# Second MLP of a hybrid decoder layer: the down projection as seven products of block sums for each 512 inner rows

## Chip, cores, metric

One core of a Trainium2 chip. The metric is the device time of one execution in microseconds, from the first to the last instruction and a little around it. Lower is better.

## Reference

One layer of a decoder, for a prompt of 2048 tokens and 32 sample tokens: an input projection with dilated attention and a state-space scan, an output projection, a cross-attention, an MLP and a final norm. What the change touches is the MLP alone:

```python
x = x + jnp.square(jax.nn.relu(rmsnorm(x, g_mlp) @ w_up)) @ w_down   # w_up 1024 x 4096, w_down 4096 x 1024
y = rmsnorm(x, g_final)
```

All data are float32. Every matmul operand is split into a high part and a low remainder, and a product is made of three matmuls: high x high, low x high, high x low.

## The kernel before

After attention and the scan, `Trunk.run` handles the tokens in two groups, one after the other: 1024 tokens (g = 0), then 1056 (g = 1, with the sample tokens). Data lie transposed: 128 features on the partitions, tokens along the free dimension. The second group's tokens are cut into three tiles of 352 (`cs`).

The MLP runs over f = 0 to 15, 256 inner rows each, and j = 0, 1. `up(f, j)` makes 128 inner rows: for each token tile 24 matmuls (`gemm`: 8 blocks of the feature dimension, three each) into a PSUM bank of the tag "g" (four banks), then `act`: DVE scales and clips (L2022), ACT squares (L2023, the high part `us[f, j, 0]`), POOL squares again (L2024) and DVE subtracts (L2025, the low part `us[f, j, 1]`), three tiles later by `line.later(3, ...)`. Then, one f behind, the half j of `down(f - 1)`: for each of four blocks m of 128 output features and each of three token tiles six matmuls (L2034 to L2036) into one of four PSUM banks (three of the tag "a", one "s", in turn), and DVE adds the bank to the running sum `xs[m]` in SBUF (L2044; L2041 and L2042 for f = 0).

`Stream` (`W`) brings the weights: `blocks()` lists them in the order of their use, 128 x 1024 values each. `load` starts the DMA from SP into one of two buffers `w_raw`; `scale` multiplies the up blocks by the norm's gain on POOL (L1335); `split` makes the parts in two halves of 512, high on ACT (`w_hi`, L1291), low on DVE (`w_lo`, L1292), into one of two buffers each. `W.next(wait)` hands out a block, starts the load of the block after the next, and through `line.later` puts the two halves of the next block's split after the tiles number `wait` and `wait + 1` of the work that begins (`line.tick()` counts tiles). `up` uses `wait` 1, `down` uses 4. Within an engine the order of the instructions is the order in which this code issues them; across engines only data and free buffers make one wait.

In the first group the attention over the sample tokens' cache (`samples`, with products on POOL in L2247 and sums on DVE in L2234) runs beside the MLP, in steps between tiles, and the down banks are three.

Of the kernel before, what the change touches and what calls it, by code (L numbers as in the profile page):

```python
# [18 lines left out]
P = 128  # L19
# [1296 lines left out]
class Stream:  # L1316


    def __init__(self, E, pool, line, blocks):
        self.E, self.pool, self.line, self.blocks = E, pool, line, list(blocks)  # L1320
        self.raw, self.parts, self.i = {}, {}, 0
        self.load(0)
        self.load(1)

    def load(self, i):
        if i < len(self.blocks):
            src, gain = self.blocks[i]
            k = src.shape[1]
            t = self.raw[i] = self.pool.tile([P, k, 1024 // k], F32, name="w_raw", tag="w_raw", bufs=2)
            self.E.nc.sync.dma_start(t, src)  # L1330

    def scale(self, i):
        if i < len(self.blocks) and self.blocks[i][1] is not None:
            t = self.raw[i]
            self.E.nc.gpsimd.tensor_tensor(t, t, self.blocks[i][1][:, :, None].to_broadcast([P, 8, P]), op=ALU.mult)  # L1335

    def split(self, i, half=None):

# [81 lines left out]
class Trunk:  # L1420
# [25 lines left out]
    def blocks(self):  # L1446
        E = self.E

        def cut(w, c, gain):
            return w.rearrange("(k p) f -> p k f", p=P)[:, :, c:c + P], gain  # L1450

        for g in range(2):
            for m in range(4):
                yield cut(E.w_in[0], 1536 + m * P, self.gm)
            for w in (E.w_mk, E.w_mv) if g == 0 else ():
                for m in range(8):
                    yield cut(w[0], m * P, None)
# [6 lines left out]
            for f in range(17):
                for j in range(2):
                    if f < 16:
                        yield cut(E.w_up[0], 256 * f + P * j, self.gu)
                    if f:
                        yield (E.w_down[0][256 * (f - 1):256 * f, 512 * j:512 * j + 512]
                               .rearrange("(k p) f -> p k f", p=P), None)  # L1470
# [36 lines left out]
    def run(self):  # L1507
# [46 lines left out]
        def group(g, tail):  # L1554
# [460 lines left out]
                    while rb2 is not None and pss:  # L2015
                        act(f, j, *pss.pop(0))

            def act(f, j, s, ps):
                k = s.stop - s.start
                t1 = small()  # L2020
# [6 lines left out]
            def down(f, m, s, w):  # L2027
# [22 lines left out]
            for f in range(16):  # L2050
                for j in range(2):
                    up(f, j)
                    if g == 0 and f == 15 and j:
# [393 lines left out]
```

## Time and profile before

| | |
|---|---|
| median of 3 runs | 3468.25 us (3466.62 to 3468.25) |
| the profiled execution | 3462.61 us, span 3460.8 us |
| PE (TensorE matmul) busy | 3297.6 us, 95% of the span |
| DVE, ACT, POOL busy | 56%, 34%, 37% |
| the second group's MLP | about 2690 to 3416 us of the span |

The trace shows for each instruction when it began and how long it took, on which engine and from which line; PEld is the weight load before a matmul. A matmul's shown duration overlaps with the next one's, so what a matmul costs is read from the distance between the starts of neighbours. "Idle before" names what ended an engine's wait. The granted clock is the share of TensorE's full clock that it was given.

### The profile page before, as it was taken

To read this page: it belongs to the slowest core of one execution; us is meant where nothing else is said; L and a number is where in the kernel's file an instruction comes from. 1 tells how busy PE (TensorE), PEld (TensorE's weight loads), DVE (VectorE), ACT (ScalarE), POOL (GpSimd) and SP (SyncE) were. 2 spreads that over 40 slices of the span, in tenths; PEclk is the share of its full clock that TensorE was granted. 3 is DMA by queue.
4 is the path that set the end of the run, shared out by engine and by line. 5 is a ranking of instruction groups with operands and counts; after the bars stand their busy time and mean duration, and the time that the engine had idled before them with its cause. 6 is when DMAs were issued, how large, how long until landed. Compare 5 with 4: busy or idle time off the path is not lost. (4 is left out here: it accounts for less than half of the span.)

```text
span 3460.8 us, 52997 instructions
## 1 busy us (share of the span) xinstructions
PE 3297.6 (95%) x20631; PEld 2926.6 (85%) x20631; DVE 1949.4 (56%) x3946; ACT 1186.5 (34%) x2764; POOL 1271.4 (37%) x1025
## 2 busy tenths in 40 slices
PE   9999998999789999899999999989999999999998
PEld 7999997777577887677776777889889999999998
DVE  5334887777664334577754455563334455555555
ACT  5443555778353333211111111344433311111113
POOL 1114555478423334766411122543324522112213
PEclk9999999999899999999999999999999999999999
DMA  7669454456772211455335423712431222222222
GB/s 205 208 192 253 102 129 142 135 142 162 222 202 71 61 49 57 166 191 198 131 127 180 158 83 111 263 40 86 128 110 37 92 98 92 96 81 98 92 96 83
DMA packets 406429, 447.25 MB, mean 129 GB/s; under 512 B 39932, under 2 KB 338607, under 8 KB 402594
## 3 DMA queue, kind: packets, MB, share of 16 engines
q1 hardware_dynamic: 375986, 384.08, 35.8%
q0 software_dynamic: 27744, 44.57, 4.8%
q10 hardware_dynamic: 2448, 15.21, 1.3%
q8 instruction: 163, 2.67, 0.3%
q14 instruction: 88, 0.72, 0.1%
HBM read 368.33 MB, written 142.44 MB: 148 GB/s over the span
## 5 line engine op out<-in xcount | busy, mean ns | idle before, releaser
L1502 PE MATMUL g_g<-g_b,w_hi 128*128 128x352 f32 (+1 forms) x1760 | 629.3, 359 | 14.8 <-ACT w_hi L1291 14.8
L1503 PE MATMUL g_g<-g_b,w_lo 128*128 128x352 f32 (+1 forms) x1760 | 621.5, 355 | 9.7 <-DVE w_lo L1292 9.7
L2024 POOL TENSOR_TENSOR g_small<-g_small 128x352 f32<-128x352 f32 (+1 forms) x160 | 143.6, 898 | 960.0 <-ACT g_a L2023 955.1
L1292 DVE TENSOR_TENSOR w_lo<-w_raw,w_hi 128x512 fp32r<-128x512 f32 x400 | 350.3, 881 | 193.2 <-ACT w_hi L1291 192.5
L1291 ACT ACTIVATE w_hi<-w_raw 128x512 fp32r<-128x512 f32 x400 | 241.1, 622 | 611.3 <-issue 354.3
L2034 PE MATMUL g_a<-g_a,w_hi 128*128 128x352 f32 (+3 forms) x1076 | 391.2, 364 | 21.7 <-DVE g_a L2044 17.8
L1502 PEld LDWEIGHTS g_g<-g_b,w_hi 128*128 128x128 f32 x1760 | 335.3, 191 | 61.4 <-ACT w_hi L1291 20.4
L2035 PE MATMUL g_a<-g_a,w_lo 128*128 128x352 f32 (+3 forms) x1076 | 385.1, 358 | 2.0 <-DVE w_lo L1292 2.0
L2036 PE MATMUL g_a<-g_a,w_hi 128*128 128x352 f32 (+3 forms) x1076 | 383.8, 357 | 0.9 <-DVE g_a L2025 0.9
L1503 PEld LDWEIGHTS g_g<-g_b,w_lo 128*128 128x128 f32 x1760 | 335.1, 190 | 41.9 <-DVE w_lo L1292 12.1
L1505 PE MATMUL g_g<-g_b,w_hi 128*128 128x352 f32 (+1 forms) x1760 | 366.7, 350 | 0.5 <-DMA g_b<-s_xl 0.5
L2044 DVE TENSOR_TENSOR g_a<-g_a,g_a 128x512 f32<-128x512 f32 (+2 forms) x504 | 292.5, 591 | 107.6 <-PE g_a L2036 106.4
L1505 PEld LDWEIGHTS g_g<-g_b,w_hi 128*128 128x128 f32 x1760 | 304.8, 188 | 31.1 <-DMA g_b<-s_xl 1.0
L2023 ACT ACTIVATE g_a<-g_small 128x352 fp32r<-128x352 f32 (+1 forms) x160 | 87.9, 551 | 635.4 <-DVE g_small L2022 635.4
L2022 DVE SCALAR_TENSOR_TENSOR g_small<-g_g,g_rb 128x352 f32<-128x352 f32 (+1 forms) x160 | 94.2, 589 | 317.0 <-PE g_g L1505 285.9
L2034 PEld LDWEIGHTS g_a<-g_a,w_hi 128*128 128x128 f32 x1076 | 202.8, 188 | 68.7 <-DVE g_a L2044 30.0
L1502 PE MATMUL g_g<-g_a,w_hi 128*128 128x352 f32 (+1 forms) x632 | 226.6, 359 | 6.5 <-ACT g_a L1571 4.6
L1503 PE MATMUL g_g<-g_a,w_lo 128*128 128x352 f32 (+1 forms) x632 | 224.4, 356 | 3.3 <-DVE w_lo L1292 3.3
L2036 PEld LDWEIGHTS g_a<-g_a,w_hi 128*128 128x128 f32 x1076 | 203.2, 189 | 23.7 <-DVE g_a L2025 1.4
L2035 PEld LDWEIGHTS g_a<-g_a,w_lo 128*128 128x128 f32 x1076 | 202.9, 189 | 22.7 <-DVE w_lo L1292 2.9
L1039 ACT ACTIVATE w_spare<-w_spare,t_stats 128x256 f32<-128x256 f32 (+1 forms) x376 | 168.7, 450 | 65.6 <-DVE t_stats L1037 65.3
L2025 DVE TENSOR_TENSOR g_a<-g_small,g_a 128x352 fp32r<-128x352 f32 (+1 forms) x160 | 186.8, 1169 | 2.6 <-POOL g_small L2024 2.4
(470 smaller groups left out, 6878.6 us busy)
## 6 DMA issues: line engine op xcount, KB each, us to landing
w_raw<-in_w_up_dram SPq DMA_DIRECT2D x64, 512.0 KB
w_raw<-in_w_down_dram SPq DMA_DIRECT2D x64, 512.0 KB
out_dram<-in_cache_win_k_dram SPq DMA_DIRECT2D x32, 1022.0 KB
out_dram<-in_cache_win_v_dram SPq DMA_DIRECT2D x32, 1022.0 KB
g_wide<-in_cache_win_k_dram SPq DMA_DIRECT2D x32, 512.0 KB
t_cf<-s_coef SPq DMA_DIRECT2D x32, 384.0 KB
g_spare<-in_cache_win_v_dram SPq DMA_DIRECT2D x48, 256.0 KB
a_xn<-in_x_prompt_dram SPq DMA_DIRECT2D x16, 512.0 KB
```

The lines of the kernel that those rows point to most:

```text
L1039: nc.scalar.activation(pr[:, u, :w], pr[:, u, :w], AF.Exp, bias=nm, scale=-1.0, accum_out=stats[:, 1, u, col:col + 1])
L1291: nc.scalar.activation(hi, src, AF.Copy)
L1292: nc.vector.tensor_tensor(lo, src, hi.bitcast(F32), op=ALU.subtract)
L1502: mm(ps[:, :n], hi[:, k], rhs[0][k][:, s], start=first and k == ks[0], stop=False)
L1503: mm(ps[:, :n], lo[:, k], rhs[0][k][:, s], start=False, stop=False)
L1505: mm(ps[:, :n], hi[:, k], rhs[1][k][:, s], start=False, stop=last and k == ks[-1])
L2024: nc.gpsimd.tensor_tensor(t1[:, :k], t1[:, :k], t1[:, :k], op=ALU.mult)
L2025: line.later(3, lambda: nc.vector.tensor_tensor(ul[:, s], t1[:, :k], uh[:, s].bitcast(F32), op=ALU.subtract))
L2034: mm(ps[:, :k], hi[:, j, c], us[f, j, 0][:, s], start=(j == 0), stop=False)
L2035: mm(ps[:, :k], lo[:, j, c], us[f, j, 0][:, s], start=False, stop=False)
L2036: mm(ps[:, :k], hi[:, j, c], us[f, j, 1][:, s], start=False, stop=(j == 1))
L2044: nc.vector.tensor_tensor(xs[m][:, s], xs[m][:, s], ps[:, :k], op=ALU.add)
```

## The change

Only the second group's MLP changes, and there f = 0 to 13. Two f are taken together as 512 inner rows. With the inner rows in two halves, the output features in two halves (512 each) and the tokens in two halves (528 each), the product is one of 2 x 2 by 2 x 2 blocks, which takes seven block products and a number of block sums instead of eight products. f = 14 and 15 stay as they were.

- `blocks()` yields, for each round of 512 inner rows, four up blocks and seven down blocks, in the order up, 1, 2, up, 5, 6, 3, up, 7, up, 4. Blocks 5, 6, 3 and 7 are sums or differences of quarters of the weights: `sums` makes them on POOL, two operations of 512 columns each, in place in `w_raw`, from the block before (`last`) or from two more halves that `load` brings into `extra`.
- `W.next` makes the sum of the next block before the load that would overwrite its source.
- `squares(p, j)` takes the place of `up`: the same matmuls, the same scaling on DVE and the square on ACT, but for p < 7 the square is kept whole, and POOL's square and DVE's subtraction fall away.
- `begin` and `rest_of` make the differences of token halves and inner halves on POOL (`combine`, 528 columns an operation); `prepare` splits an operand into its parts, high on ACT, low on POOL.
- `product(ends, shared)` is one of the seven: 4 blocks of 128 output features x 2 tiles of 264 tokens, six matmuls each, into the same four banks; DVE adds the bank to each of the running sums named in `ends`, and for blocks 1 and 6 to a sum `common`, which three quarters of the output get at the end. Blocks 1, 5 and 7 so have two targets for each bank.
- `whole` puts the residual into `xs` on POOL during the first round, where f = 0 did it with its first addition.
- The split of a next block's halves stands after the first and the second tile in `product` (`wait` 1).

The running sums and prepared operands lie in tiles that the MLP of the second group did not use. The number of matmuls goes from 14 x 144 = 2016 of 352 columns to 7 x 7 x 48 = 2352 of 264 columns.

```diff
+                else:
+                    for f in range(8):
+                        for j, then in enumerate(("12", "563", "7", "4")):
+                            yield cut(E.w_up[0], 512 * f + P * j, self.gu)
...
+    def sums(self, i, kind):
+        t = self.raw[i]
+        for k in range(2):
+            d = t[:, k]
+            o = self.last[:, k] if kind in "63" else self.extra[k]
+            a, b = (o, d) if kind == "6" else (d, o)
+            op = ALU.add if kind == "5" else ALU.subtract
+            self.E.nc.gpsimd.tensor_tensor(d, a, b, op=op)
+        self.last = t
...
         self.split(i)
+        if wait is not None:
+            self.scale(i + 1)
         self.load(i + 2)
...
+                def prepare(src):
+                    hi, lo = sets[ready[0] % 2]
+                    ready[0] += 1
+                    for k in range(2):
+                        nc.scalar.activation(hi[:, k].bitcast(F32R), src[k], AF.Copy)
+                        nc.gpsimd.tensor_tensor(lo[:, k].bitcast(F32R), src[k], hi[:, k], op=sub)
...
+                def product(ends, shared=None, hooks={}):
+                    hi, lo = W.next()
+                    bh, bl = (t.bitcast(F32R) for t in sets[turn[0] % 2])
...
+                    for i in range(8):
+                        m, c = divmod(i, 2)
+                        f, t = slice(P * m, P * m + P), slice(264 * c, 264 * c + 264)
+                        ps = psum("aaas"[i % 4])[:, :264]
+                        for k in range(2):
+                            mm(ps, hi[:, k, f], bh[:, k, t], start=k == 0, stop=False)
+                            mm(ps, lo[:, k, f], bh[:, k, t], start=False, stop=False)
+                            mm(ps, hi[:, k, f], bl[:, k, t], start=False, stop=k == 1)
+                        line.tick()
+                        for mh, th in ends:
+                            o = 528 * th + 264 * c
+                            add_to(xs[4 * mh + m][:, o:o + 264], ps)
...
+                    squares(p, 0, {0: [lambda: prepare(part(old, 1, 0))]})
+                    product([(0, 0)], "first" if p == 1 else "more")
+                    product([(0, 0)], None, {1: [lambda: prepare(both(ta))]})
+                    squares(p, 1, {0: [lambda: prepare(both(tb))], 1: [lambda: W.scale(W.i + 1)],
+                                   2: [lambda: rest_of(old)]})
+                    product([(0, 1), (1, 1)], None, {6: [lambda: W.scale(W.i + 1)]})
+                    product([], "more", {1: [lambda: prepare(part(old, 1, 1))]})
+                    product([(0, 1)], None, {1: [lambda: prepare(both(tb))]})
+                    squares(p, 2, {0: []})
+                    product([(1, 0), (1, 1)], None, {1: []})
+                    squares(p, 3, {0: [lambda: prepare(both(ta))]})
+                    product([(1, 0)], None, {1: [lambda: begin(new)] if p < 7 else [],
+                                             4: [lambda: prepare(part(new, 0, 0))] if p < 7 else []})
```

On DVE, before: the end of an up and the begin of a down half. L2022 is the scaling of a tile, L2025 the low part of the squares, L2044 the addition of a bank (g_a_..., g_s_...) to a running sum (g_a04 is `xs[4]`), L1292 half of a w_lo.

```order
L2022 SCALAR_TENSOR_TENSOR g_small_25799<-g_g_25772,g_rb2_24954 128x352
L2022 SCALAR_TENSOR_TENSOR g_small_25828<-g_g_25803,g_rb2_24954 128x352
L2025 TENSOR_TENSOR g_a13_25738<-g_small_25768,g_a12_25737 128x352
L2044 TENSOR_TENSOR g_a04_25415<-g_a04_25415,g_s_25835 128x352
L2025 TENSOR_TENSOR g_a13_25738<-g_small_25799,g_a12_25737 128x352
L2044 TENSOR_TENSOR g_a04_25415<-g_a04_25415,g_a_25844 128x352
L2025 TENSOR_TENSOR g_a13_25738<-g_small_25828,g_a12_25737 128x352
L2044 TENSOR_TENSOR g_a04_25415<-g_a04_25415,g_a_25853 128x352
L1292 TENSOR_TENSOR w_lo_25870<-w_raw_25735,w_hi_25869 128x512
L2044 TENSOR_TENSOR g_a05_25449<-g_a05_25449,g_a_25862 128x352
```

The same place on DVE now: the end of a `squares` (L2178 is its scaling) and the begin of product 1. L2123 is the addition; g_sum is `common`.

```order
L2178 SCALAR_TENSOR_TENSOR g_small_24867<-g_g_27213,g_rb2_24977 128x352
L2178 SCALAR_TENSOR_TENSOR g_small_24868<-g_g_27242,g_rb2_24977 128x352
L1292 TENSOR_TENSOR w_lo_27280<-w_raw_27175,w_hi_27279 128x512
L2123 TENSOR_TENSOR g_a00_24872<-g_a00_24872,g_a_27272 128x264
L2123 TENSOR_TENSOR g_sum_24886<-g_sum_24886,g_a_27272 128x264
L1292 TENSOR_TENSOR w_lo_27280<-w_raw_27175,w_hi_27279 128x512
L2123 TENSOR_TENSOR g_a00_24872<-g_a00_24872,g_a_27285 128x264
L2123 TENSOR_TENSOR g_sum_24886<-g_sum_24886,g_a_27285 128x264
L2123 TENSOR_TENSOR g_a01_24873<-g_a01_24873,g_a_27296 128x264
L2123 TENSOR_TENSOR g_sum_24886<-g_sum_24886,g_a_27296 128x264
```

The w_lo halves have moved from behind the third addition of a half to ahead of the first two tiles' additions, and each bank is now read twice.

On POOL, before: one f and a half of the second group. L2024 is the square of a tile, L1335 the scaling of an up block.

```order
L2024 TENSOR_TENSOR g_small_27828<-g_small_27828 128x352
L2024 TENSOR_TENSOR g_small_27859<-g_small_27859 128x352
L2024 TENSOR_TENSOR g_small_27888<-g_small_27888 128x352
L1335 TENSOR_TENSOR w_raw_27795<-w_raw_27795,g_gu_7428 128x1024
L2024 TENSOR_TENSOR g_small_28034<-g_small_28034 128x352
L2024 TENSOR_TENSOR g_small_28065<-g_small_28065 128x352
L2024 TENSOR_TENSOR g_small_28094<-g_small_28094 128x352
L1335 TENSOR_TENSOR w_raw_28001<-w_raw_28001,g_gu_7428 128x1024
```

On POOL now, from product 2 to product 6 of one round: L2120 is the low part of a prepared operand (g_wide is a prepared set or `ta`, g_sum is `tb`), L1346 a block sum, L2113 a difference (`rest_of`), L1358 the scaling.

```order
L1358 TENSOR_TENSOR w_raw_25382<-w_raw_25382,g_gu_7428 128x1024
L2120 TENSOR_TENSOR g_wide_24881<-g_wide_24884,g_wide_24880 128x528 x2
L1346 TENSOR_TENSOR w_raw_25465<-w_raw_25465,g_small_24870 128x512
L1346 TENSOR_TENSOR w_raw_25465<-w_raw_25465,g_small_24871 128x512
L2120 TENSOR_TENSOR g_wide_24883<-g_sum_24885,g_wide_24882 128x528 x2
L1346 TENSOR_TENSOR w_raw_25543<-w_raw_25465,w_raw_25543 128x512 x2
L2113 TENSOR_TENSOR g_wide_24884<-g_a12_25094,g_sum_24885 128x528
L2113 TENSOR_TENSOR g_wide_24884<-g_a13_25188,g_sum_24885 128x528
L2113 TENSOR_TENSOR g_sum_24885<-g_a12_25094,g_a10_24891 128x528
L2113 TENSOR_TENSOR g_sum_24885<-g_a13_25188,g_a11_25000 128x528
L1346 TENSOR_TENSOR w_raw_25644<-w_raw_25644,w_raw_25543 128x512 x2
L2120 TENSOR_TENSOR g_wide_24881<-g_a12_25094,g_wide_24880 128x528
```

POOL's three squares for each up are gone, and a row of operations on two SBUF tiles has taken their place.

## Rows read from the trace of the kernel before

**Rows 1.** The page's first part: busy time of each engine, share of the span, instructions.

```profile
PE 3297.6 (95%) x20631; PEld 2926.6 (85%) x20631; DVE 1949.4 (56%) x3946; ACT 1186.5 (34%) x2764; POOL 1271.4 (37%) x1025
```

**Rows 2.** Busy time by stretch: the begin of the second group's MLP, and its steady part.

```profile
core 0: us, PE busy (x) PEld busy (x) DVE busy (x) ACT busy (x) POOL busy (x), PEclk, DMA share, GB/s
...
2690.00:2744.00 54.00, 49.94 (x293) 47.80 (x292) 22.84 (x38) 17.89 (x28) 22.47 (x22) 0.97 0.24 79
2744.00:3395.00 651.00, 650.99 (x4056) 650.69 (x4055) 364.32 (x618) 107.47 (x198) 139.24 (x127) 1.00 0.27 91
```

**Rows 3.** Groups of instructions by line in 2744 to 3395: line, engine, operation, out<-in, form, count | busy us, mean ns | idle before, what ended it.

```profile
L2044 DVE TENSOR_TENSOR g_a<-g_a,g_a 128x352 f32<-128x352 f32 x243 | 121.9, 514 | 36.0 <-PE g_a L2036 35.8
...
L2025 DVE TENSOR_TENSOR g_a<-g_small,g_a 128x352 fp32r<-128x352 f32 x84 | 89.3, 1063 | 0.0
L1292 DVE TENSOR_TENSOR w_lo<-w_raw,w_hi 128x512 fp32r<-128x512 f32 x113 | 83.3, 737 | 36.8 <-ACT w_hi L1291 36.8
L1291 ACT ACTIVATE w_hi<-w_raw 128x512 fp32r<-128x512 f32 x113 | 67.9, 624 | 263.9 <-issue 179.2 <-POOL w_raw L1335 84.7
L2024 POOL TENSOR_TENSOR g_small<-g_small 128x352 f32<-128x352 f32 x85 | 65.9, 775 | 510.2 <-ACT g_a L2023 510.2
L1335 POOL TENSOR_TENSOR w_raw<-w_raw,g_gu 128x1024 f32<-128x1024 f32 x28 | 61.0, 2180 | 0.0
```

**Rows 4.** The first group's MLP, timeline (start us, duration us, engine, line): a w_lo beside a POOL product, the addition behind it, and PE.

```profile
1504.24 2.84 POOL L2247 TENSOR_TENSOR g_spare<-g_wide,g_spare 128x1024 f32<-128x1024 f32 x1
...
1505.35 2.28 DVE L1292 TENSOR_TENSOR w_lo<-w_raw,w_hi 128x512 fp32r<-128x512 f32 x1
...
1507.56 0.67 DVE L2044 TENSOR_TENSOR g_a<-g_a,g_a 128x512 f32<-128x512 f32 x1
...
1508.28 0.50 PE L2034 MATMUL g_a<-g_a,w_hi 128*128 128x512 f32 x1 [0.58 <-DVE g_a L2044]
1508.62 0.39 PE L2035 MATMUL g_a<-g_a,w_lo 128*128 128x512 f32 x1
```

**Rows 5.** The first group's MLP in three views: busy time of 1470 to 1710 (columns as in rows 2); PE's waits there (us in total, times, longest); DVE's groups by line in 1440 to 1700.

```profile
1470.00:1710.00 240.00, 225.17 (x950) 176.23 (x949) 180.25 (x199) 35.71 (x60) 152.36 (x70) 1.00 0.53 178
...
PEld g_a L2034 <- DVE g_a L2044: 22.9, 21, 1.6
...
L1292 DVE TENSOR_TENSOR w_lo<-w_raw,w_hi 128x512 fp32r<-128x512 f32 x43 | 52.8, 1229 | 13.4 <-ACT w_hi L1291 13.4
...
L2044 DVE TENSOR_TENSOR g_a<-g_a,g_a 128x512 f32<-128x512 f32 x76 | 50.1, 677 | 11.2 <-PE g_a L2036 11.2
```

**Rows 6.** Timeline of PE in an earlier stage: matmuls of 256 columns back to back.

```profile
376.69 1.12 PE L480 MATMUL s_psg<-s_x,w_hi 128*128 128x256 f32 x8
377.65 0.28 PE L477 MATMUL s_psg<-s_x,w_hi 128*128 128x256 f32 x1
```

**Rows 7.** Timelines of the second group's MLP: DVE operations back to back; the last matmul of a down tile, the next tile's first one and DVE's addition; a scaling with ACT's square and the w_hi behind it.

```profile
2735.56 0.51 DVE L2041 TENSOR_TENSOR g_a<-g_a,g_b 128x352 f32<-128x352 f32 x1
2735.99 0.51 DVE L2041 TENSOR_TENSOR g_a<-g_s,g_b 128x352 f32<-128x352 f32 x1
2736.42 1.50 DVE L2041 TENSOR_TENSOR g_a<-g_a,g_b 128x352 f32<-128x352 f32 x3
...
2849.28 0.68 DVE L1292 TENSOR_TENSOR w_lo<-w_raw,w_hi 128x512 fp32r<-128x512 f32 x1
2849.88 0.51 DVE L2044 TENSOR_TENSOR g_a<-g_a,g_a 128x352 f32<-128x352 f32 x1
...
2859.92 0.53 DVE L2022 SCALAR_TENSOR_TENSOR g_small<-g_g,g_rb 128x352 f32<-128x352 f32 x1 [2.41 <-PE g_g L1505]
...
2860.48 0.50 ACT L2023 ACTIVATE g_a<-g_small 128x352 fp32r<-128x352 f32 x1 [3.69 <-DVE g_small L2022]
2860.89 0.61 ACT L1291 ACTIVATE w_hi<-w_raw 128x512 fp32r<-128x512 f32 x1
...
2899.98 0.32 PE L2036 MATMUL g_a<-g_a,w_hi 128*128 128x352 f32 x1
...
2900.14 0.32 PE L2034 MATMUL g_a<-g_a,w_hi 128*128 128x352 f32 x1
...
2900.34 0.52 DVE L2044 TENSOR_TENSOR g_a<-g_a,g_a 128x352 f32<-128x352 f32 x1 [0.44 <-PE g_a L2036]
```

**Rows 8.** POOL's groups by line in 2600 to 3461 (columns as in rows 3), and the scaling's durations there (minimum, median, maximum in ns).

```profile
L1730 POOL TENSOR_TENSOR g_wide<-g_b 128x1056 f32<-128x1056 f32 x6 | 15.3, 2546 | 0.0
L2121 POOL TENSOR_TENSOR g_wide<-g_wide,g_gf 128x512 f32<-128x512 f32 x7 | 9.1, 1324 | 11.7 <-ACT g_wide L2120 11.7
L2085 POOL TENSOR_TENSOR g_acc<-g_acc,g_small 128x512 f32<-128x512 f32 x6 | 7.8, 1297 | 16.4 <-ACT g_small L2083 16.1
...
L1335 POOL TENSOR_TENSOR w_raw<-w_raw,g_gu x32: 1896/2179/2182, 2673.4 to 3378.0; 128x1024 f32<-128x1024 f32 x32
```

**Rows 9.** Timelines of POOL and DVE in the second group's MLP: a scaling and a subtraction that met it, and the same subtraction without.

```profile
2846.36 2.18 POOL L1335 TENSOR_TENSOR w_raw<-w_raw,g_gu 128x1024 f32<-128x1024 f32 x1
...
2844.94 0.52 DVE L2025 TENSOR_TENSOR g_a<-g_small,g_a 128x352 fp32r<-128x352 f32 x1
...
2847.14 1.78 DVE L2025 TENSOR_TENSOR g_a<-g_small,g_a 128x352 fp32r<-128x352 f32 x1
```

**Rows 10.** Timeline of PE after the first up of the second group's MLP.

```profile
2714.08 0.42 PE L1502 MATMUL g_g<-g_b,w_hi 128*128 128x352 f32 x1 [3.54 <-ACT w_hi L1291]
```

More of the change, by code (lines that the diff above doesn't have):

```diff
@@ L1321, in __init__ @@
         self.raw, self.parts, self.i = {}, {}, 0
+        self.scaled, self.extra = set(), None
         self.load(0)
@@ L1327, in load @@
             src, gain = self.blocks[i]
+            if isinstance(src, tuple):
+                src, kind, more = src
+                if more is not None:
+                    for k in range(2):
+                        self.E.nc.sync.dma_start(self.extra[k], more[:, k])
             k = src.shape[1]
@@ L1330, in load @@
             self.E.nc.sync.dma_start(t, src)
-    def scale(self, i):
-        if i < len(self.blocks) and self.blocks[i][1] is not None:
+    def sums(self, i, kind):
[7 more added lines that the diff above has]
+        self.last = t
+    def scale(self, i):
+        if i in self.scaled or i >= len(self.blocks):
+            return
+        self.scaled.add(i)
+        src, gain = self.blocks[i]
+        if isinstance(src, tuple):
+            self.sums(i, src[1])
+        elif gain is not None:
             t = self.raw[i]
-            self.E.nc.gpsimd.tensor_tensor(t, t, self.blocks[i][1][:, :, None].to_broadcast([P, 8, P]), op=ALU.mult)
+            self.E.nc.gpsimd.tensor_tensor(t, t, gain[:, :, None].to_broadcast([P, 8, P]), op=ALU.mult)
     def split(self, i, half=None):
@@ L1463, in blocks, with down @@
                 yield cut(E.w_xo[0], m * P, None)
[L1464 to L1470, printed above, removed]
+            def down(f, j):
+                return E.w_down[0][256 * f:256 * f + 256, 512 * j:512 * j + 512].rearrange("(k p) f -> p k f", p=P), None
+            if g == 0:
+                for f in range(17):
+                    for j in range(2):
+                        if f < 16:
+                            yield cut(E.w_up[0], 256 * f + P * j, self.gu)
+                        if f:
+                            yield down(f - 1, j)
+            else:
+                for f in range(8):
+                    for j, then in enumerate(("12", "563", "7", "4")):
+                        yield cut(E.w_up[0], 512 * f + P * j, self.gu)
+                        for i in then if f else "":
+                            part = lambda mk: down(2 * (f - 1) + mk % 10, mk // 10)[0]
+                            at, more = {"1": (0, None), "2": (1, None), "5": (10, 11), "6": (0, None), "3": (1, None),
+                                        "7": (0, 10), "4": (11, None)}[i]
+                            yield (part(at) if i in "124" else (part(at), i, None if more is None else part(more))), None
+                for f in (14, 15):
+                    for j in range(2):
+                        yield down(f, j)
     def open(self):
@@ L2016, in up, with act @@
                         act(f, j, *pss.pop(0))
-            def act(f, j, s, ps):
+            def act(f, j, s, ps, t1=None):
                 k = s.stop - s.start
-                t1 = small()
+                if t1 is None:
+                    t1 = small()
                 uh, ul = us[f, j, 0], us[f, j, 1]
@@ L2049, in group @@
                 side.append(samples(E, spare, lambda: psum("s")))
-            for f in range(16):
+            else:
+                bilinear()
+            for f in range(16 if g == 0 else 0):
                 for j in range(2):
```

96 lines of the change are left out of this document (added).

## The prediction

> **What bounds the kernel now.** I read the page first: PE is busy for 95% of the span [rows 1]. Then the stretches of the second group's MLP: from 2744 to 3395 us PE is busy for 650.99 of 651.00 us at granted clock 1.00, with 4056 matmuls, one every 0.1605 us; DVE is busy for 56% and POOL for 21% of it [rows 2]. The reader should see that nothing but PE's own work sets the end here, so that a matmul taken away is worth its full spacing, and that PE has no slack at all: any new wait is paid in full. The groups by line then give the prices of what stands beside PE [rows 3], and a stretch of the first group's MLP, where DVE and POOL are busier, shows what PE loses when they are late [rows 4, 5].
>
> **PE: what is saved.** Inner rows 0 to 3583 are f = 0 to 13. Before, each f costs 8 x 3 tiles x 6 = 144 matmuls of 352 columns: 2016 x 0.1605 = 323.6 us. After, seven rounds of seven products of 8 tiles x 6 = 48 make 2352 matmuls of 264 columns. No row has 264; 256 columns come every 0.120 us (eight of them in 376.69 to 377.65) [rows 6], and 352 every 0.1605, so 0.00042 us for a column and 0.1234 us for 264: 290.2 us. The saving is 33.4 us, **4.77 us for each round**; a tile takes 0.74 us and a product 5.92. A spacing of 0.122 or 0.125 would move the saving by 3 us. The ups (`squares`), f = 14 and 15 and everything outside the second MLP keep their matmuls.
>
> **DVE, POOL, ACT: what is added, and what of it hides.** In each round (four `squares`, seven products) DVE has 22 weight subtractions (w_lo) against 16 in two f before, 80 additions or copies of 264 columns against 48 of 352, 12 scalings, and no more L2025. Back to back DVE takes 0.43 us for 352 columns (2735.56, 2735.99, 2736.42) and 0.60 for 512 (2849.28 to 2849.88) [rows 7], so 0.34 for 264: 22 x 0.60 + 80 x 0.34 + 12 x 0.43 = 45.6 us of the round's 46.2 (288 up matmuls) + 41.5 (products) = 87.7 us of PE. ACT gets 22 w_hi at 0.62, 12 squares at 0.50 and 14 copies of 528 columns at about 0.64: 29 us. POOL gets 4 scalings at 2.18 [rows 3], 8 block sums of 512 columns and 22 operations of 528 columns (14 remainders, 8 differences) at 1.30 and 1.33, from 1297 and 1324 ns for 512 [rows 8], and loses its squares: 48 us. DMA brings 11 weight blocks and two extra halves for a round instead of 8 blocks, against a DMA share of 0.27 [rows 2]. By busy time everything hides. What decides is the order on DVE, so I follow that.
>
> **The first cost: three products with two targets, right after a `squares`.** They are 1, 5 and 7 in the code's numbers. Each PSUM tile is there added twice (0.68 us of DVE against 0.74 of PE), there are four banks, and two w_lo of the next weight block stand ahead of the first and second tile's additions on DVE. Counted from the end of the `squares`: DVE's scaling starts 0.20 us after PE could go on (a last matmul at 2899.98, DVE at 2900.34, matmul spacing 0.16) and takes 0.53; ACT's square follows, its next instruction (w_hi) 0.41 later, and takes 0.62 [rows 7]. So the first w_lo starts at 1.8 us, the first tile's two additions end at 3.2, and PE, which wants that bank back at 4 x 0.74 = 2.96, waits 0.27; the second w_lo and two additions end at 4.46, and PE, due at 4.08, waits 0.43. A restart costs 0.11 more (1508.28 to 1508.62 instead of 0.23 apart) [rows 4]. That is 0.9 us, and **2.8 us for a round**. Before, the same chain was covered: the down half's first w_lo stands behind four tiles.
>
> **The second cost: w_lo against POOL.** At 2846.36 POOL starts a scaling of 2.18 us; a DVE subtraction from two SBUF tiles begun at 2847.14 then takes 1.78 instead of 0.52 and ends 0.38 us after POOL does [rows 9]. In the first group a w_lo took 2.28 us under a POOL product, the addition behind it came late and PE waited 0.58 [rows 4]; there 43 w_lo had a mean of 1229 ns, while additions from PSUM kept 677 [rows 5]. So a w_lo that meets a POOL operation ends about 0.55 us after that operation; additions don't care. POOL is now in work exactly beside some products: in 2 it makes the remainders for 5 (their buffers come free when 1 ends), in 5 it is still at the differences put behind the sum for 6, in 6 it makes the remainders for 3, and in 4 it starts the differences of the next round. Worked as above, with POOL operations of 1.3 us back to back, each of these four loses 0.5 to 1.8 us, since DVE arrives there already late or has only four banks of 0.74 behind it. A bound from below is zero: the w_lo falls into gaps, or is first (then POOL waits). The bound from above is both w_lo held for a whole 1.3 us and 0.1 to restart twice, less the slack of 0.5: 2.2. I take 0.85 for each, nearest to the first group's row, where PE waited 22.9 us in 21 times, 1.1 each [rows 5]: **3.4 us for a round**, with 0 and 8.8 as ends.
>
> **The last round and the ends.** In round 7 the squares go through `act` as before: 12 more two-input subtractions on DVE beside the doubled products, 12 POOL squares, but no differences for a next round: +2 us (0 to 6). At the end twelve additions of the shared sum join down(14), where DVE had a tile of 0.97 us for 0.43: nothing, up to 1. At the start eight POOL additions of 1056 columns at 2546 ns [rows 8] replace 24 short ones and hide under four `squares` of 11.6 us. I put +1 for both.
>
> **Sum.** 7 x (2.8 + 3.4 - 4.77) + 2 + 1 = +13 us; rounded for the spread of the second cost, +12. The profiled execution took 3462.61 us (span 3460.8) and the median is 3468.25, so 5.6 us over the profile; I add the change to the median: **3480 us, 0.35% slower**. What this kernel's measurement can tell from no change is about 0.2%, 7 us.
>
> **Rivals.**
> *Faster: POOL does not meet w_lo.* If the second cost is absent, because the w_lo come first or POOL runs ahead into the `squares`, a round gains 4.77 - 2.8 = 2.0 us, and with 3 us for the last round and the ends the whole comes to -11: 3457 us. It decides from a second cost of under 0.5 us for a round; below 1.5 there is still some gain. For it: w_lo in this stretch now has a mean of 737, not 1229 [rows 3, 5], POOL is idle for half the time. Against: POOL's work in 2, 6 and 4 is released by the same events that start DVE's.
> *No change: the second cost is about half of mine.* With 1.5 us (0.5 to 2.5) a round loses 4.3 of the 4.77, and the last round and the ends take the rest: 3468 (3461 to 3475).
> *Far slower: POOL's row becomes the bound.* The block sums, remainders and differences form one line on POOL from product 2 to product 3; the remainders for 3 are ready, as I count, only 1.3 us before PE wants them. If POOL operations stretch by 15%, as the scaling does (1.90 us at least, 2.18 mostly [rows 8]), the line is 3 us late in every round, a third of which the wait inside 6 already holds: +14, so 3494.
> *The clock.* In the stretch 2690 to 2744, in which PE waited 3.54 us for a weight half [rows 10], the granted clock was 0.97 [rows 2], that is some 3.2 us at 1.2 GHz; in 1470 to 1710, with 21 waits of up to 1.6 us, it stayed at 1.00 [rows 5]. If PE dropped once in a round for as long, it would lose 1.6 us each time, 11 in all: 3491. The Trainium skill (TensorE: Matmul & The Clock Gate, A second HAM failure mode: psum-queue depth-cycling) says that short idles between groups of matmuls that cycle through PSUM banks can make the clock fall again and again; the trace's stretch with bank waits does not bear that out, so it gets little.
>
> **How the numbers follow.** Forecast (3475 to 3488) 0.37; no change 0.25; faster 0.25; POOL the bound 0.09; the clock 0.04. The range reaches from 3455, just past the faster rival, to 3498, past the POOL rival and short of the upper end of the second cost (7 x (8.8 - 3.4) = +38 on the forecast), which would need every w_lo held; some 0.2 stay outside. Faster by over 0.2%: 0.25; within: 0.25; slower: the other three, 0.50.
>
> **What would show it.** Matmuls of 264 columns about 0.123 us apart, 2352 of them. PE waiting on DVE's additions in the products, and nearly not in the `squares`: some 6 us in a round of about 94 us, seven times. Of these waits those in 1, 5 and 7 at the fifth and sixth tile, without POOL; those in 2, 5, 6 and 4 behind a w_lo of over 1.1 us that ends 0.55 us after a POOL operation. DVE busy for under 65%, POOL for some 55%, the granted clock at 1.00. I am wrong if w_lo keep to 0.7 us (faster), if PE waits for the remainders on POOL rather than for DVE (POOL the bound), if 264 columns come at another spacing, or if the fourth bank comes back sooner than counted.

## Result and the profile after

The changed kernel took **3496.99 us** (median of 4 runs, 3495.02 to 3499.07) beside 3467.43 us before (3461.97 to 3468.25): ratio 1.0089, interval 1.0071 to 1.0106, that is 29.6 us slower. The forecast was 3480 us, 12 us slower: the direction and the kind of loss came out as forecast, the size did not. The profiled execution took 3496.41 us with a span of 3494.6, against 3460.8 before, so the trace shows 33.8 us of difference, 7.2 of them ahead of the second group's MLP, which begins at 2692.7 instead of 2685.5 us.

The first row is the page's busy time [rows 1]; the others are busy times by stretch [rows 2]: one steady stretch of 94 us, and products 1, 7 and 4 of the last round.

```profile
PE 3283.8 (94%) x20967; PEld 2896.8 (83%) x20967; DVE 1978.5 (57%) x4136; ACT 1259.8 (36%) x2904; POOL 1505.6 (43%) x1139
```

```profile
core 0: us, PE busy (x) PEld busy (x) DVE busy (x) ACT busy (x) POOL busy (x), PEclk, DMA share, GB/s
...
2842.00:2936.00 94.00, 88.18 (x617) 86.08 (x616) 54.47 (x114) 25.71 (x48) 51.16 (x34) 1.00 0.34 118
...
3325.00:3342.00 17.00, 14.97 (x106) 14.54 (x105) 13.86 (x32) 3.77 (x7) 7.15 (x5) 0.90 0.48 165
...
3387.00:3398.00 11.00, 7.75 (x49) 7.22 (x48) 6.89 (x18) 1.65 (x3) 2.63 (x2) 0.84 0.37 144
...
3410.00:3421.00 11.00, 8.18 (x51) 7.59 (x50) 8.64 (x14) 1.73 (x4) 7.30 (x5) 0.85 0.14 48
```

PE, busy for 650.99 of 651.00 us before [rows 2], now has almost 6 us without work in 94, and DVE and POOL are busy for 58% and 54%: no engine is full. Who makes PE wait, from 2744 to 3320 us (rounds 1 to 6), is seen in the waits (us in total, times, longest) and in the groups by line (columns as in [rows 3]):

```profile
PEld g_a L2136 <- DVE g_a L2123: 33.7, 44, 1.1
PE g_a L2136 <- DVE g_a L2123: 24.0, 40, 0.9
PEld g_a L2136 <- DVE g_sum L2123: 12.9, 16, 1.3
```

```profile
L1292 DVE TENSOR_TENSOR w_lo<-w_raw,w_hi 128x512 fp32r<-128x512 f32 x133 | 128.2, 964 | 86.2 <-ACT w_hi L1291 86.2
...
L1358 POOL TENSOR_TENSOR w_raw<-w_raw,g_gu 128x1024 f32<-128x1024 f32 x24 | 48.2, 2009 | 21.7 <-DVE g_small L2178 10.1 <-issue 6.5 <-DMA g_small<-in_w_down_dram 3.7
```

What PE waits for is DVE's addition (L2123) that gives a bank back; 1.2 us more are the copy that stands in its place in round 1 (L2146). A w_lo has gone from 737 ns [rows 3] to 964.

All of it lies inside the products. The four `squares` of a round take 11.47 us each, with every matmul at the 0.16 us of before; a product is timed from its first matmul to the first one behind it. In us, rounds 2 to 6 (mean) and round 7:

| product | 1 | 2 | 5 | 6 | 3 | 7 | 4 | sum |
|---|---|---|---|---|---|---|---|---|
| rounds 2 to 6 | 7.48 | 6.75 | 7.69 | 6.76 | 5.96 | 6.81 | 7.97 | 49.42 |
| round 7 | 9.99 | 5.85 | 10.53 | 5.77 | 6.51 | 10.97 | 10.67 | 60.29 |

A product in which PE never waits takes 5.82 us; two f of before took 288 x 0.1605 = 46.2. So a normal round loses 3.2 us, the last 14.1. Round 3 shows the two kinds of loss. First its product 1, timelines of PE, POOL, ACT and DVE (start, duration, engine, line; idle before and what ended it):

```profile
2944.47 0.29 PE L2136 MATMUL g_a<-g_wide,w_hi 128*128 128x264 f32 x1
...
2945.20 0.28 PE L2136 MATMUL g_a<-g_wide,w_hi 128*128 128x264 f32 x1
...
2948.23 0.39 PE L2136 MATMUL g_a<-g_wide,w_hi 128*128 128x264 f32 x1 [0.66 <-DVE g_sum L2123]
...
2949.51 0.39 PE L2136 MATMUL g_a<-g_wide,w_hi 128*128 128x264 f32 x1 [0.28 <-DVE g_sum L2123]
...
2945.05 1.90 POOL L1358 TENSOR_TENSOR w_raw<-w_raw,g_gu 128x1024 f32<-128x1024 f32 x1 [3.28 <-issue]
...
2945.63 1.14 ACT L1291 ACTIVATE w_hi<-w_raw 128x512 fp32r<-128x512 f32 x2
...
2946.28 1.22 DVE L1292 TENSOR_TENSOR w_lo<-w_raw,w_hi 128x512 fp32r<-128x512 f32 x1 [1.09 <-ACT w_hi L1291]
2947.42 0.42 DVE L2123 TENSOR_TENSOR g_a<-g_a,g_a 128x264 f32<-128x264 f32 x1
2947.76 0.41 DVE L2123 TENSOR_TENSOR g_sum<-g_sum,g_a 128x264 f32<-128x264 f32 x1
2948.10 0.68 DVE L1292 TENSOR_TENSOR w_lo<-w_raw,w_hi 128x512 fp32r<-128x512 f32 x1
```

Two tiles begin 0.73 us apart: six matmuls at 0.122. The first w_lo starts 1.81 us after the product, as the forecast's chain had it, but meets POOL's scaling, which ends at 2946.95: it ends at 2947.50, 0.55 later. Neither of the two reads or writes a buffer of the other, so data and free buffers do not explain this wait; without POOL's part it is gone (run 5). Below, such a pair is said to meet. Both additions of the first tile stand behind it, and PE's fifth tile, due at 2947.40, begins at 2948.23; its sixth waits for the second w_lo in the same way. Then product 4 of the same round:

```profile
3019.12 2.61 POOL L2113 TENSOR_TENSOR g_wide<-g_a 128x528 f32<-128x528 f32 x2
3021.70 3.04 POOL L2113 TENSOR_TENSOR g_sum<-g_a,g_wide 128x528 f32<-128x528 f32 x2
...
3021.82 1.75 DVE L1292 TENSOR_TENSOR w_lo<-w_raw,w_hi 128x512 fp32r<-128x512 f32 x1 [1.08 <-ACT w_hi L1291]
3023.49 0.42 DVE L2123 TENSOR_TENSOR g_a<-g_a,g_a 128x264 f32<-128x264 f32 x1
3023.83 1.45 DVE L1292 TENSOR_TENSOR w_lo<-w_raw,w_hi 128x512 fp32r<-128x512 f32 x1
...
3023.97 0.39 PE L2136 MATMUL g_a<-g_wide,w_hi 128*128 128x264 f32 x1 [0.85 <-DVE g_a L2123]
...
3025.68 0.39 PE L2136 MATMUL g_a<-g_wide,w_hi 128*128 128x264 f32 x1 [0.72 <-DVE g_a L2123]
```

Here each bank is added once, but both w_lo meet POOL's differences. The second ends at 3025.28, 0.54 us after POOL's pair.

In the last round product 7 looks like this (L2065 is POOL's square, L2066 the square's low part, L2063 the scaling of a tile):

```profile
3388.75 0.77 POOL L2065 TENSOR_TENSOR g_small<-g_small 128x352 f32<-128x352 f32 x1 [3.04 <-ACT g_a L2064]
3389.48 1.90 POOL L1358 TENSOR_TENSOR w_raw<-w_raw,g_gu 128x1024 f32<-128x1024 f32 x1
...
3391.41 1.15 ACT L1291 ACTIVATE w_hi<-w_raw 128x512 fp32r<-128x512 f32 x2 [2.74 <-POOL w_raw L1358]
...
3392.07 0.69 DVE L1292 TENSOR_TENSOR w_lo<-w_raw,w_hi 128x512 fp32r<-128x512 f32 x1 [3.50 <-ACT w_hi L1291]
...
3393.50 0.39 PE L2136 MATMUL g_a<-g_wide,w_hi 128*128 128x264 f32 x1 [3.03 <-DVE g_a L2123]
...
3396.04 0.42 PE L2136 MATMUL g_a<-g_wide,w_hi 128*128 128x264 f32 x1
3396.26 0.42 PE L2137 MATMUL g_a<-g_wide,w_lo 128*128 128x264 f32 x1
```

POOL's squares are back in this round and wait for ACT, and the scaling of the last up block is queued behind them: w_hi, w_lo and the additions follow, and PE stands still for 3.03 us. After that matmuls come 0.22 us apart for a while, at the lower of the two clock levels (1.2 GHz); the granted clock of the stretch is 0.84. The same follows the long waits in products 1, 5 and 4 of this round. In the four products together 47 distances more than in another round are near 0.22 us instead of 0.12, some 4.7 us by a count in the trace. So of the 10.9 us that the last round loses beyond another, over four tenths are matmuls at the lower level; most of the rest are longer waits.

And product 5 of the last round: a square's low part and the w_lo behind it are both held by POOL's differences.

```profile
3355.21 3.34 POOL L2113 TENSOR_TENSOR g_wide<-g_a,g_sum 128x528 f32<-128x528 f32 x2
...
3356.40 0.95 DVE L2066 TENSOR_TENSOR g_a<-g_small,g_a 128x352 fp32r<-128x352 f32 x1
3357.28 1.82 DVE L1292 TENSOR_TENSOR w_lo<-w_raw,w_hi 128x512 fp32r<-128x512 f32 x1
...
3359.83 0.59 PE L2136 MATMUL g_a<-g_wide,w_hi 128*128 128x264 f32 x1 [2.31 <-DVE g_a L2123]
```

### The profile page after: what moved, and what is told of

Its sections match the earlier page's. It is cut to its first block, busy times and chain, and to the rows that moved or that the text cites. A ratio compares the mean times of both kernels' runs of the same rounds, so it can differ in the third digit from the quotient of the medians.

```text
span 3494.6 us, 54569 instructions
## 1 busy us (share of the span) xinstructions
PE 3283.8 (94%) x20967; PEld 2896.8 (83%) x20967; DVE 1978.5 (57%) x4136; ACT 1259.8 (36%) x2904; POOL 1505.6 (43%) x1139
## 5 line engine op out<-in xcount | busy, mean ns | idle before, releaser
L1292 DVE TENSOR_TENSOR w_lo<-w_raw,w_hi 128x512 fp32r<-128x512 f32 x442 | 416.2, 946 | 258.5 <-ACT w_hi L1291 257.7
L2065 POOL TENSOR_TENSOR g_small<-g_small 128x512 f32<-128x512 f32 (+1 forms) x76 | 78.3, 1031 | 449.6 <-ACT g_a L2064 449.5
L2075 PE MATMUL g_a<-g_a,w_hi 128*128 128x512 f32 (+3 forms) x572 | 228.2, 399 | 22.0 <-DVE g_a L2085 18.2
L2076 PE MATMUL g_a<-g_a,w_lo 128*128 128x512 f32 (+3 forms) x572 | 222.3, 389 | 1.9 <-DVE w_lo L1292 1.9
L2077 PE MATMUL g_a<-g_a,w_hi 128*128 128x512 f32 (+3 forms) x572 | 221.6, 387 | 0.9 <-DVE g_a L2066 0.9
L2136 PE MATMUL g_a<-g_wide,w_hi 128*128 128x264 f32 x588 | 177.0, 301 | 46.1 <-DVE g_a L2123 32.9
L2085 DVE TENSOR_TENSOR g_a<-g_a,g_a 128x512 f32<-128x512 f32 (+3 forms) x270 | 174.9, 658 | 74.0 <-PE g_a L2077 73.2
L2064 ACT ACTIVATE g_a<-g_small 128x512 fp32r<-128x512 f32 (+1 forms) x76 | 46.4, 610 | 373.1 <-DVE g_small L2063 373.1
L2138 PE MATMUL g_a<-g_wide,w_hi 128*128 128x264 f32 x588 | 168.9, 287 | 0.0
L2137 PE MATMUL g_a<-g_wide,w_lo 128*128 128x264 f32 x588 | 168.7, 287 | 0.0
L2075 PEld LDWEIGHTS g_a<-g_a,w_hi 128*128 128x128 f32 x572 | 108.2, 189 | 70.3 <-DVE g_a L2085 30.8
L1848 POOL TENSOR_SCALAR g_small<-g_small,g_den 128x256 f32<-128x256 f32 x64 | 58.9, 929 | 244.9 <-DVE g_den L1846 244.9
```

What stands on the lines that cost most here:

```text
L1292: nc.vector.tensor_tensor(lo, src, hi.bitcast(F32), op=ALU.subtract)
L2075: mm(ps[:, :k], hi[:, j, c], us[f, j, 0][:, s], start=(j == 0), stop=False)
L2076: mm(ps[:, :k], lo[:, j, c], us[f, j, 0][:, s], start=False, stop=False)
L2077: mm(ps[:, :k], hi[:, j, c], us[f, j, 1][:, s], start=False, stop=(j == 1))
L2136: mm(ps, hi[:, k, f], bh[:, k, t], start=k == 0, stop=False)
L2138: mm(ps, hi[:, k, f], bl[:, k, t], start=False, stop=k == 1)
```

## The experiments

**Theory A**: the loss is the order on DVE. A w_lo stands ahead of the additions that PE needs first; this costs by itself where a `squares` went before (first cost), and more where POOL holds the w_lo (second cost). **Theory B**: POOL's line of sums, differences and remainders sets the pace, wherever w_lo stands. Times are medians; the kernel before took 3465.3 us beside the first four runs, 3465.96 beside the next four, 3466.01 beside the last. Products are again in us, mean of rounds 2 to 6.

**1. The split of the next weight block behind the fourth and fifth tile.**

```diff
-                    hi, lo = W.next()
+                    hi, lo = W.next(4)
```

Expected: 

> In the seven products the two halves of the next weight block's split stand behind the fourth and fifth tile (wait 4) instead of behind the first and second; nothing else changes. Theory A (the loss is the order on DVE: a w_lo stands ahead of the additions that PE needs first): the waits at the fifth and sixth tile, 8.4 us in each of rounds 1 to 6, are gone but for at most 1 us, and of the 11 us that round 7 loses beyond that some 5 stay; 3497 - 6 x 7.8 - 7 = 3443 us (3436 to 3452), faster than before. Theory B (POOL's line of sums, differences and remainders sets the pace, and a w_lo that meets POOL is late wherever it stands): the waits move to the ends of the products, where PE then waits for w_lo, w_hi or the remainders; 3485 to 3500 us.

Measured: 3441.84 us, ratio 0.9923 (0.9911 to 0.9935): faster than before by 23.5 us. A round's products take 42.21 us instead of 49.42, the last round's 50.59. Theory A holds, theory B falls: POOL does exactly what it did, in the same order, and PE does not wait for it. (The edit moves ACT's w_hi too, but PE's waits had been for DVE.) Only product 5 (6.81) and product 6 (6.12) still lose more than 0.1. The wait in front of product 6:

```profile
2869.83 3.06 POOL L2113 TENSOR_TENSOR g_sum<-g_a,g_a 128x528 f32<-128x528 f32 x2
...
2870.51 1.19 DVE L1292 TENSOR_TENSOR w_lo<-w_raw,w_hi 128x512 fp32r<-128x512 f32 x1
...
2872.30 1.14 DVE L1292 TENSOR_TENSOR w_lo<-w_raw,w_hi 128x512 fp32r<-128x512 f32 x1
2873.36 2.12 DVE L2123 TENSOR_TENSOR g_a<-g_a,g_a 128x264 f32<-128x264 f32 x6
...
2874.26 0.36 PE L2136 MATMUL g_a<-g_wide,w_hi 128*128 128x264 f32 x1 [0.83 <-ACT g_wide L2119]
```

The profile names ACT, but the bank of product 6's first tile is that of product 5's fifth, whose two additions are the first of the six from 2873.36 and end near 2874.1. What ACT wrote just then is the operand of product 3; that of product 6 had been made from 2861.51 on. Run 9 tests it.

**2. POOL quiet but for the scaling** (all of it from round 2 on, in part already in round 1; the operations below stood without a condition).

```diff
+                        if ready[0] < 5:
                             nc.gpsimd.tensor_tensor(lo[:, k].bitcast(F32R), src[k], hi[:, k], op=sub)
...
+                    for k in range(2 if p < 2 else 0):
                         nc.gpsimd.tensor_tensor(dst[:, k], a[k], b[k], op=op)
...
+            if i < 30:
                 self.E.nc.gpsimd.tensor_tensor(d, a, b, op=op)
```

Expected: 

> Leaves out, from round 2 on, POOL's block sums of weights, its differences of token and inner halves, and the remainders of the prepared operands, so that the output is that of stale operands; PE, DVE and ACT issue what they did, and w_lo keep their place ahead of the first two tiles. Theory A with both costs as predicted: with POOL quiet only the first cost is left, about 0.9 us in each of products 1, 5 and 7, and products 2, 6 and 4 lose at most 0.2 each; a round loses 3 us instead of 8.4, and w_lo have a mean near 690 ns instead of 952; rounds 2 to 6 give 5 x 5.4 = 27 us, round 7 some 4: 3466 us (3460 to 3472). If the order on DVE does it all without POOL: no change, 3490 or more. If POOL's row alone does it: all waits gone, some 3450.

Measured: 3476.08 us, above the expected range, and the products say why: 2 and 4 fell to 5.96 and 6.14, 5 to 6.81, as expected, but 1 stayed at 7.39 and 6 rose to 7.31. The scaling of the up blocks was still on POOL and met the w_lo of these two. The list of meetings in the prediction had left this POOL operation out. Run 5 takes it away too.

**3. The split moved only in products 1, 5 and 7.**

```diff
-                    hi, lo = W.next()
+                    hi, lo = W.next(4 if len(ends) + bool(shared) > 1 else 1)
```

Expected: 

> The split stands behind the fourth and fifth tile only in the three products with two additions for each bank (1, 5 and 7); in 2, 6, 3 and 4 it stays behind the first and second. Theory A: the waits of 1, 5 and 7 (1.68, 1.88 and 0.98 us) go, those of 2, 6 and 4 (0.92, 0.92, 2.13) stay; 4.5 us less in a round, 6 x 4.5 = 27 and some 4 to 6 in round 7: 3465 us (3458 to 3472). Theory B: the same waits at the ends of 1, 5 and 7, 3490 to 3500.

Measured: 3472.86 us, just above the range. 1 and 7 are free of waits (5.86, 5.81), 5 lost 0.98 instead of 1.87, 4 kept its 7.96. Product 6 also gained (6.12), since DVE no longer arrives late, and product 3 lost 1.1 (6.89) that it had not lost before. That was not foreseen; the trace of product 3, which begins at 2879.94, shows it:

```profile
2879.84 1.90 POOL L1358 TENSOR_TENSOR w_raw<-w_raw,g_gu 128x1024 f32<-128x1024 f32 x1
...
2881.77 1.15 ACT L1291 ACTIVATE w_hi<-w_raw 128x512 fp32r<-128x512 f32 x2 [4.65 <-POOL w_raw L1358]
...
2882.44 0.69 DVE L1292 TENSOR_TENSOR w_lo<-w_raw,w_hi 128x512 fp32r<-128x512 f32 x1 [1.87 <-ACT w_hi L1291]
```

A w_lo that comes 2.5 us into a product because its input is late does the same harm as one that POOL holds.

**4. One addition for each bank in 1, 5 and 7.**

```diff
-                        for mh, th in ends:
+                        for mh, th in ends[:1]:
...
-                        if shared:
+                        if shared and (p == 1 or not ends):
```

Expected: 

> Leaves out the second addition of each bank in products 1, 5 and 7 (for product 1 from round 2 on), so that part of the output lacks these products; w_lo keep their place. If the doubled additions are needed for the first cost: product 7 (1.8 + 0.53 + 0.34 us after the squares is under four tiles of 0.73) loses nothing instead of 0.98, 1 and 5 lose what the meeting with POOL costs, 0.8 and 1.1 instead of 1.68 and 1.88, and 2 and 6, which DVE then reaches in time, 0.5 instead of 0.92; some 3.4 us less in a round: 3473 us (3466 to 3480). If it is the chain and the two w_lo alone: no change, 3490 or more.

Measured: 3475.6 us, inside the range. Product 7 fell from 6.81 to 6.13, 1 to 6.65, 2 and 6 to 5.84; 5 kept 7.37, and 3 rose to 6.58. So the second addition is needed for most of the first cost, and for what products 2 and 6 lose, but not for the waits that POOL makes in 5 and 4. In 2 and 6 it takes both: here POOL still works, and they lose nothing.

**5. POOL silent: the scaling left out as well.** To run 2 is added:

```diff
-        elif gain is not None:
+        elif gain is not None and (i < 20 or self.extra is None):
```

Expected: 

> As the run before with POOL's sums, differences and remainders left out, and now POOL's scaling of the up blocks by the gain as well (the output is that of stale and unscaled operands); in that run the scaling was still there, and products 1 and 6 still lost 1.3 and 1.5 us. If it is POOL as such that stretches w_lo: products 1 and 6 of rounds 2 to 6 fall to 6.8 and at most 6.1 us, w_lo to a mean of about 690 ns, a round of products to 44.5 us, only products 1, 5 and 7 lose about 0.95 each (the first cost alone); 3468 us (3462 to 3473). If products 1 and 6 lose by DVE's own order: they stay at 7.3, 3476.

Measured: 3456.66 us, ratio 0.9972 (0.9959 to 0.9985), below the expected range, in part because round 7 fell too, to 51.66. A round's products take 44.30. The w_lo of 2842 to 3300 us:

```profile
L1292 DVE TENSOR_TENSOR w_lo<-w_raw,w_hi 128x512 fp32r<-128x512 f32 x112 | 77.3, 690 | 65.0 <-ACT w_hi L1291 65.0
```

690 ns again. Products 1, 5 and 7 take 6.81 us each: 0.99 too much, the first cost alone. Products 2, 6 and 4 lose 0.14, 0.14 and 0.31. What POOL's meetings cost, with the second additions in place, is the difference to the changed kernel: 0.67 in product 1, 0.79 in 2, 0.88 in 5, 0.80 in 6, 0.14 in 3, nothing in 7 and 1.84 in 4: 5.1 us for a round.

**6. Both: the split moved, and two edits in the last round** (those of runs 7 and 8).

Expected: 

> The split behind the fourth and fifth tile, and two edits in the last round: the subtractions that make the squares' low parts wait for the tiles of the next up block, where DVE has time, and the scaling of the last up block stands behind the first POOL square of its predecessor instead of behind the third. Theory A: the last round's products take 43 to 45 us instead of 50.6, other rounds stay at 42.2: 3434 us (3430 to 3439). Rival (the last round is late for POOL's squares as such): 3440 to 3444.

Measured: 3435.82 us, ratio 0.9907 (0.9891 to 0.9924); the last round's products take 44.71, 5.9 less than in run 1. This version is faster than both kernels; its interval overlaps that of run 1, so that the gain over run 1 is seen in the products and not in the time.

**7. The last round's low parts later.**

```diff
-                line.later(3, lambda: nc.vector.tensor_tensor(ul[:, s], t1[:, :k], uh[:, s].bitcast(F32), op=ALU.subtract))
+                line.later(late, lambda: nc.vector.tensor_tensor(ul[:, s], t1[:, :k], uh[:, s].bitcast(F32), op=ALU.subtract))
...
-                                act(f, jj, s, ps, t1)
+                                act(f, jj, s, ps, t1, (19, 27, 11, 11)[j])
```

Expected: 

> The changed kernel with one edit in the last round: its twelve subtractions on DVE (the squares' low parts) stand at the tiles of the next up block instead of three tiles behind their own, that is, no longer among a product's first additions. If they are what the last round loses: products 1, 5 and 4 of that round fall from 9.99, 10.53 and 10.67 to some 7.5, 7.7 and 8.0 us, product 7 stays over 10; 3489 us (3485 to 3492). If POOL's squares or TensorE's clock by itself make the last round long: 3495 to 3499.

Measured: 3491.13 us. The last round's products take 55.08 instead of 60.29: 1, 5 and 4 fell to 8.00, 7.40 and 7.06, product 7 stayed at 10.88; 2, 6 and 3 gave 3.6 of it back. The time alone would not show the effect, here and in run 8: the ratios to the kernel before (1.0054 to 1.0084, and 1.0056 to 1.0086) overlap that of the changed kernel.

**8. The last scaling earlier.**

```diff
-                    squares(p, 2, {0: []})
+                    squares(p, 2, {0: [lambda: W.scale(W.i + 1)] if p == 7 else []})
```

Expected: 

> The changed kernel with one other edit in the last round: POOL scales the last up block behind the first of the three squares of the up block before, instead of behind all three, so that ACT's w_hi in product 7 does not wait for it. Expected: product 7 of the last round falls from 10.97 to some 8.5 us, all else stays; 3494 us (3491 to 3497). If the wait is ACT's own row of squares: no change.

Measured: 3492.24 us; product 7 of the last round took 7.79 instead of 10.97. Its two waits:

```profile
3387.35 0.39 PE L2136 MATMUL g_a<-g_wide,w_hi 128*128 128x264 f32 x1 [0.34 <-DVE g_a L2123]
3389.07 0.39 PE L2136 MATMUL g_a<-g_wide,w_hi 128*128 128x264 f32 x1 [0.74 <-DVE g_a L2123]
```

That all else stays was not so. Rounds 1 to 6 are the code of the changed kernel, and still product 1 of round 6 took 9.40 us (7.75 there) and product 4 of round 1 took 9.49 (7.96 there). In both, 17 or 18 distances are near 0.22 us, behind waits of at most 1.25 us. The stretch with that product 1, columns as in [rows 2]:

```profile
3226.00:3240.00 14.00, 12.48 (x87) 12.06 (x86) 11.53 (x26) 3.76 (x7) 4.15 (x3) 0.88 0.24 75
```

**9. The split moved and POOL silent** (runs 1 and 5 together).

Expected: 

> The split behind the fourth and fifth tile, and POOL's sums, differences, remainders and scalings of the second MLP left out (the output is that of stale operands). With the split moved alone, product 5 still lost 1.0 us at its end and product 6 0.3, put down by the profile to ACT's high part of a prepared operand. Theory A: it is two w_lo of 1.1 to 1.2 us that POOL stretches, and DVE's doubled additions behind them; without POOL, products 5 and 6 of every round take 5.8 to 5.9 us, a round's products 41.0: 1.2 us less in each of rounds 2 to 6, and some 3 to 6 in round 7: 3432 us (3428 to 3437). If ACT's high part is the cause: product 5 stays at 6.8.

Measured: 3430.51 us; products 5 and 6 take 5.85 and 5.91 us, a round's products 40.93. So the two waits that run 1 left were w_lo held by POOL, not ACT's prepared operand, which ACT still makes here, and 40.9 us is what seven products cost when nothing waits.

## Why the prediction was wrong in size

- **What bounds the kernel**: right. PE had no slack, and every wait in a product came out in the time.
- **The saving**: a little low. 264 columns come every 0.1215 us, not 0.1234; a round saves 46.2 - 40.7 = 5.5 us, not 4.77 (40.9 measured in run 9).
- **The first cost** (products 1, 5 and 7 behind a `squares`): right in place, mechanism and size. 2.8 us forecast, 3 x 0.99 = 3.0 measured without POOL, at the fifth and sixth tile. Run 4 shows that the doubled additions are needed for it, run 1 that moving the split takes it away. Products 2, 6 and 4 lose another 0.6 by the same order, which had been put at nothing.
- **The second cost** is the first step that failed: "I take 0.85 for each", for products 2, 5, 6 and 4, 3.4 in all. For 2, 5 and 6 the size was right (0.79, 0.88, 0.80), which is luck in part: it had been picked between 0 and 2.2. Product 4 cost 1.84, near the bound of 2.2: it too follows a `squares`, and both its w_lo meet POOL. And product 1 was missing (0.67): POOL's four scalings had been counted as busy time and given no place. Together 5.1.
- **The last round** is the second: "+2 us (0 to 6)" against 10.9 more than another round. The twelve extra DVE subtractions are ahead of the first additions and meet POOL (run 7: 5.2 us); the twelve POOL squares, taken only as work, tie POOL to PE's pace, so that a scaling that elsewhere runs ahead comes late (run 8: 3.2 us in product 7). Both figures hold a part that is the clock: the lower level behind the long waits, some 4.7 us of the 10.9, had no place in this term, and it is gone from a product when its long wait is. The rest, some 2.5 us, was not taken apart. POOL's four additions of the shared sum, which the prediction had hidden under down(14), run in product 4 of this round:

```profile
3411.92 6.57 POOL L2224 TENSOR_TENSOR g_a<-g_a,g_sum 128x528 f32<-128x528 f32 x4
...
3413.99 1.78 DVE L1292 TENSOR_TENSOR w_lo<-w_raw,w_hi 128x512 fp32r<-128x512 f32 x1
...
3416.16 0.39 PE L2136 MATMUL g_a<-g_wide,w_hi 128*128 128x264 f32 x1 [2.26 <-DVE g_a L2123]
```

  They are what the low parts and w_lo meet there, but not the rest: in run 7 they run in the same place without the low parts, and product 4 takes 7.06 us, less than in another round.

- **The ends**: "I put +1 for both", but the begin gained 5.1 us: the first 360 matmuls from the begin of the second group's MLP took 60.0 us instead of 65.1. Before, POOL's scaling stood behind three squares, w_hi behind the scaling, and PE waited 3.54 us [rows 10]; without the squares the scaling runs ahead, and no wait there is over 0.30 us. POOL before, then POOL and PE now:

```profile
2709.27 2.24 POOL L2024 TENSOR_TENSOR g_small<-g_small 128x352 f32<-128x352 f32 x3 [20.33 <-ACT g_a L2023]
2711.47 1.90 POOL L1335 TENSOR_TENSOR w_raw<-w_raw,g_gu 128x1024 f32<-128x1024 f32 x1
...
2708.65 1.91 POOL L1358 TENSOR_TENSOR w_raw<-w_raw,g_gu 128x1024 f32<-128x1024 f32 x1
...
2718.38 0.43 PE L1543 MATMUL g_g<-g_b,w_lo 128*128 128x352 f32 x1 [0.30 <-DVE w_lo L1292]
```

The sum against the forecast's 13 us (12 when rounded): saving 7 x 0.7 = 5 us better, the order on DVE 7 x 0.8 = 6 worse, POOL's meetings 7 x 1.7 = 12 worse, the last round 9 worse, the begin 6 better; that makes 29. From its first up matmul to its last down matmul the MLP of the second group took 781.2 us instead of 755.1 in the two profiles, 26.1 more; the 3 us between were not taken apart. The 7.2 us ahead of the MLP are in code that the change leaves alone: in the profiles of the nine runs the MLP begins at 2686.3 to 2695.3 us. The medians lie 29.6 apart.

- **Rivals.** *POOL does not meet w_lo, 3457*: it did not happen, but run 5 made it happen and measured 3456.66. The sign of this change does hang on the second cost, as the rival said; its parts differ (more saved for a round, more lost in the last), so that the two figures agree is luck. *POOL's row the bound*: no; PE never waited for POOL's operands, and run 1 is 55 us faster with the same row. *The clock*: in rounds 1 to 6 the granted clock stayed at 1.00 with waits of up to 1.1 us. In the last round it fell in four products and cost some 0.9 to 1.5 us in each, near the rival's 1.6. The Trainium skill (TensorE: Matmul & The Clock Gate, A second HAM failure mode: psum-queue depth-cycling) says that short idles between groups of matmuls that cycle through PSUM banks can make the clock go up and down; the first six rounds of the changed kernel are such cycling and do not show it, the same code in run 8 shows it twice.

## What to carry to other kernels

A wait ahead of an addition that frees a bank is paid by the matmul engine as soon as it is longer than the banks last. So when tiles get shorter (0.73 us here for 0.97), look first at what the code puts ahead of the first additions of a block, and move the next block's preparation behind as many tiles as there are banks: one number in the code turned 0.9% slower into 0.8% faster. Give every operation of a helper engine a place in the order, not only a share of its busy time: two errors of this prediction, in product 1 and in the last round, are operations that were counted and not placed.

## What the runs showed of the hardware

- A DVE subtraction of two SBUF tiles of 512 columns that meets a POOL operation on SBUF ended 0.55 and 0.54 us after POOL's in the two rows above, one of 352 columns 0.38 after it in [rows 9]. A DVE addition with one operand in PSUM took 0.41 to 0.43 us whatever POOL did. The Trainium skill (SBUF — State Buffer, Who interferes with whom) says that a DVE instruction with two SBUF inputs and a GpSimd instruction that reads SBUF cannot run together and that the second to start waits for the whole of the first; runs 5 and 9 agree, with w_lo at 690 and 686 ns when POOL is silent against 949 in the changed kernel from 2842 to 3300 us.
- POOL loses as well. A remainder of 528 columns took 1.33 us with no w_lo beside it; a pair of them, mostly with a w_lo between, took 3.00 to 3.22 us in round 3.
- After waits of 1.7 to 3.0 us in the last round PE went on at matmuls 0.22 us apart, the lower clock level, for some 10 to 15 matmuls (granted clock 0.84 to 0.90 in the three stretches shown). The length of the wait does not tell by itself: in run 8 the same followed a wait of 1.25 us (granted clock 0.88) and, in product 4 of round 1, waits of 0.85 and 0.72 us, behind which PE went on at the full level in the other rounds; in run 7 it did not follow a wait of 1.65 us in product 1 of round 1.
- The cause that the profile names for a wait can be the wrong one: PE's 0.83 us in front of product 6 stood under ACT and was DVE's, as run 9 bears out.
